# A hybrid decoder step: the split of the memory states per weight unit, the query pass ahead of the update, and the heads' work beside the projection on other places

## The chip, the cores and the metric

The kernel runs on one core of a Trainium2 chip. The metric is device time in microseconds (us) from start to end of one execution; lower is better. Engines are named TensorE (PE in the rows, PEld for its weight loads), VectorE (DVE), ScalarE (ACT), GpSimd (POOL) and SyncE (SP, which here only issues DMAs). Each engine works through its own instructions in the order in which the program emitted them.

## The reference

One layer on 576 tokens (512 of a new sequence, 64 of 8 running sequences with 8 new tokens each): a projection of 2048 inputs to 8 x 1024 columns and 8 gates, four heads of a chunked linear attention with a 256 x 256 state each, a gated convolution of width 31, an output projection and a layer norm. What matters for the change is the attention of the 8 running sequences, whose states come from memory (8 sequences x 4 heads, 256 x 256 float32 each):

```python
proj = jnp.einsum('bsd,de->bse', x, w_in) + b_in
q, k, v, o, zm, ga, gg, zc, ig, fg = jnp.split(proj, SPLITS, axis=-1)
...
s = jnp.einsum('bhtd,bhsd->bhts', qc, kc) * jnp.exp(dmat - m_t[..., None])
num = (w_inter[..., None] * jnp.einsum('bhtd,bhde->bhte', qc, C)     # queries meet the old state
       + jnp.einsum('bhts,bhse->bhte', s, vc))
...
C_new = decay[..., None, None] * C + jnp.einsum('bhs,bhsd,bhse->bhde', ws, kc, vc)   # update
```

## The kernel before, in words

**The projection sets the pace.** The 64 column blocks of 128 are made one after the other. The first three come from a loop of their own; the other 61 are called steps here and counted from 4. A step is 16 k-steps, one for each 128 rows of the weights, and a k-step is six matmuls (L185: float32 data in two parts, high and low, three products for each of two spans of tokens). Four k-steps share one weight unit of 512 columns, which `split` makes from the loaded `raw`: ScalarE the high part `whi` (L86), then VectorE the low part `wlo` (L87). It is called at the first k-step of a unit for the unit three ahead, and every second call then issues SyncE's load of another 512 KB of weights.

**All other work stands beside the projection**, at places written by hand: `at(s, k, f, ...)` has `f` emitted behind the matmuls of k-step k of step s (k may pass 16 and then counts on into later steps). A table sets the places for each head h, counted from a base step: `b_E` to `b_q` prepare the scores and the keys of the head (in the words of the change, its front), `b_rep` to `b_shT` are its back part.

**The states.** For each head the 8 states are taken in two groups of four (r = 0, 1). They lie in `Ct` tiles, 8 buffers, loaded by `c_load` (L377, SyncE). `c_split` cuts a state into three bfloat16 parts: c0 = round(C) (ScalarE, L401), the rest cr = C - c0 (VectorE, L407), c1 = round(cr) (ScalarE, L399), c2 = cr - c1 (VectorE, L404). It is called in two halves: part 0 emits the two ScalarE operations (c1 of the state before and c0 of this one), part 1, two k-steps later, the two of VectorE. One state follows another every four k-steps.

- `b_qC` (L640): 24 small matmuls of the queries with the three parts of four states, into one PSUM tile `mi`, which ScalarE then copies to `nsb` (L642).
- `b_sKV` (L652): 8 small matmuls, the update of four states, into three `mi` tiles and `ns`; VectorE adds them to the decayed states (`Ct`, L657) and GpSimd issues the stores (`o_cs`, L658).
- `b_sLN` part 0 (L667): the tokens' own scores times values, into one `mi`.
- `b_kT` (L502): the keys' transposes, two calls, one `mi` each.
- `c_next`: the loads of the next head's four states, into the buffers just stored.

There are three `mi` buffers, taken in turn by all of these. The parts c0 and c1 lie in the buffers that held the scores `Ph` and `Pl`; for head 0's second group alone they lie in four other buffers. In the first group the update (24 k-steps behind the first score product) stands ahead of `b_sLN` (26) and the query pass (28); in the second the update (49 for head 0, 46 for the others) stands ahead of the query pass (51).

**Also in these engines' queues:** `b_E` has GpSimd add the mask (L444) for the next head and ScalarE take the exponential (L439). `b_parts` splits q and k (L455, L456); the projection's result for k leaves PSUM through ScalarE (L201). At steps 25 to 30 the gates o and zm follow the heads: ScalarE's sigmoid (L799), for zm a VectorE product (L805), then a GpSimd product (L816, L820).

Of the kernel before, what the change touches and what calls it, by code (L numbers as in the profile page):

```python
# [7 lines left out]
F32 = mybir.dt.float32  # L8
F32R = mybir.dt.float32r
BF16 = mybir.dt.bfloat16  # L10
AF = mybir.ActivationFunctionType
# [3 lines left out]
P = 128  # L15
# [3 lines left out]
NB, T8 = 8, 8  # L19
# [37 lines left out]
def hybrid(ctx, tc, x0, wg0, wu, wgate, cpack, gpack, sct, hist, xres, lnp,  # L57
           o_y, o_ys, o_C, o_m, o_cs, o_ns, o_ms, o_cv, o_cvs):
    nc = tc.nc
    pe, act, dve, pool = nc.tensor, nc.scalar, nc.vector, nc.gpsimd  # L60
# [4 lines left out]
    def mt(shape, dt, name, tag=None, bufs=None):  # L65
        return main.tile(shape, dt, name=name, tag=tag or name, bufs=bufs or 1)
# [43 lines left out]
    CT = mt([P, NCT, NH], F32, "CT")  # L110
# [5 lines left out]
    hT = {}  # L116
# [37 lines left out]
    def mi(shape=(P, 512)):  # L154
        return psum.tile(list(shape), F32, name="mi", tag="mi", bufs=3)
# [111 lines left out]
    for k in range(KT):  # L267
        for n, x in enumerate((XH, XL)):
            for b in range(2):
                c0, c1 = SPANS[b]  # L270
# [99 lines left out]
    m = {}  # L370
    CS = {}
# [4 lines left out]
            CS[i] = m["t"]([P, 2, 258], F32, "Ct", bufs=8)  # L376
            nc.sync.dma_start(CS[i], sct[i])  # L377

    def c_split(h, r, j, part):

        i = NB * h + 4 * r
        if (j, part) == (0, 0):
            if (h, r) == (0, 1):
                for n in ("c0", "c1"):
                    m[n] = [mt([P, 2, 2, 258], BF16, n, tag="hT", bufs=8) for _ in range(2)]
            else:
                for n, tag in (("c0", "Ph"), ("c1", "Pl")):
                    c = m["t"]([P, 4, 2, 258], BF16, n, tag=tag)  # L390
                    m[n] = [c[:, :2], c[:, 2:]]
            c = m["t"]([P, 4, 2, 258], BF16, "c2")
            m["c2"] = [c[:, :2], c[:, 2:]]
            m["cr"] = {}
        c0, c1, c2 = (lambda j, c=m[n]: c[j // 2][:, j % 2] for n in ("c0", "c1", "c2"))
        cr = m["cr"]
        if part == 0:
            if j:
                act.activation(c1(j - 1), cr[j - 1], AF.Copy)  # L399
            if j < 4:  # L400
                act.activation(c0(j), CS[i + j], AF.Copy)  # L401
        else:
            if j:
                dve.tensor_sub(c2(j - 1), cr.pop(j - 1), c1(j - 1))  # L404
            if j < 4:
                cr[j] = m["t"]([P, 2, 258], F32, "cr", bufs=2)
                dve.tensor_sub(cr[j], CS[i + j], c0(j))  # L407

    def rb_load(h):
        m["RB"] = m["t"]([P, TOK + TS], F32, "RB")  # L410
# [181 lines left out]
    def rsqrt(r, v, a):  # L592

        act.activation(r, v, AF.Ln)
        act.activation(r, r, AF.Exp, scale=-0.5)
        dve.tensor_mul(a, r, r)
        dve.tensor_mul(a, a, v)
        dve.tensor_scalar(a, a, -0.5, 1.5, op0=OP.mult, op1=OP.add)
        dve.tensor_mul(r, r, a)

    def head_ln(num, rows, n, thr):
        t = m["t"]
        sm = t([rows, 5, n], F32, f"sm{n}")
        st = t([rows, n, 6], F32, f"st{n}")
        mv = t([rows, n, 2], F32, f"mv{n}")
        ad, rd, v, r, a = (sm[:, i] for i in range(5))
        den = num[:, :, 256]
        for i in range(n):
            dve.bn_stats(st[:, i], num[:, i, :DH])
        for i in range(n):  # L610
            dve.bn_aggr(mv[:, i], st[:, i])
        dve.scalar_tensor_tensor(ad, den, -1.0, den, op0=OP.mult, op1=OP.max)
        dve.tensor_tensor(ad, ad, thr, op=OP.max)
        dve.reciprocal(rd, ad)
        dve.tensor_mul(v, mv[:, :, 1], rd)
        dve.tensor_mul(v, v, rd)
        dve.tensor_scalar(v, v, EPS, None, op0=OP.add)
        rsqrt(r, v, a)
        dve.tensor_mul(r, r, rd)
        for i in range(n):  # L620
            dve.tensor_scalar(num[:, i, :DH], num[:, i, :DH], mv[:, i, 0:1], r[:, i:i + 1],
                              op0=OP.subtract, op1=OP.mult)
# [9 lines left out]
    def b_qC(h, r):  # L632

        if r == 0:
            m["nsb"] = m["t"]([P, 2, 258], F32, "nsb")
        ps = mi()
        for d in range(2):
            for n in ("c0", "c1", "c2"):
                for j in range(4):
                    pe.matmul(ps[32 * j:32 * j + 32, :258], lhsT=m["Q"][:, d, 4 * r + j], rhs=m[n][j // 2][:, j % 2, d],  # L640
                              start=d == 0 and n == "c0", stop=d == 1 and n == "c2")
        act.activation(m["nsb"][:, r], ps[:, :258], AF.Copy)  # L642
        if r:
            act.dma_start(nsd[h].rearrange("j i t r e -> (j i t) r e"), m["nsb"])
# [48 lines left out]
    def at(s, k, f, *a):  # L693
        s, k = s + k // KT, k % KT
        beside.setdefault((s, k), []).append((f, a))
# [4 lines left out]
    at(6, 9, open_m)  # L700
    for h in range(NH):
        b = 6 * h + 1
        o = 2 if h == 0 else 0
        for i in range(4):
            at(b + 3 + o, (14 + i if h == 0 else 7 + 2 * i), b_E, h, i)
        at(6 if h == 0 else b + 2, 11 if h == 0 else 5, b_parts, "q", h)
        at(6 if h == 0 else b + 4, 13 if h == 0 else 0, b_parts, "k", h)
        at(b + 4 + o, 5, b_QK, h, 0)
        at(b + 4 + o, 7, b_QK, h, 1)
        at(b + 4 + o, 7, b_rep, "k", h)  # L710
        at(b + 4 + o, 9, b_kT, h, 0)
        at(b + 4 + o, 11, b_kT, h, 1)
        at(b + 4 + o, 13, b_stk, "k", h)
        at(b + 4 + o, 14, b_q, h)
        if h + 1 < NH:
            at(b + 7, 0, rb_load, h + 1)
        o = 14 if h == 0 else 0
        at(b + 6, o + 1, b_rep, "v", h)
        at(b + 6, o + 2, b_vT, h, 0)
        at(b + 6, o + 4, b_vT, h, 1)  # L720
        at(b + 6, o + 6, b_stk, "v", h)
        at(b + 6, o + 7, b_vs, h)
        at(b + 6, o + 9, b_sn, h)
        o = (b + 6, o + 10)
        for I in range(4):
            at(o[0], o[1] + 2 * I, b_SV, h, I)
        at(o[0], o[1] + 7, lambda h: head_ln(m["num"], P, 4, CT[:, 14:18, h]), h)
        at(o[0], o[1] + 8, b_KV, h, 0)
        at(o[0], o[1] + 10, b_KV, h, 1)
        at(o[0], o[1] + 14, b_hT, h, 0)  # L730
        at(o[0], o[1] + 16, b_hT, h, 1)
        for r, k in enumerate((8, 30 if h == 0 else 29)):
            for j in range(5):
                for part in range(2):
                    at(o[0], o[1] + k + 4 * j + 2 * part, c_split, h, r, j, part)
            at(o[0], o[1] + (24, 49 if h == 0 else 46)[r], b_sKV, h, r)
            at(o[0], o[1] + (28, 51)[r], b_qC, h, r)
            at(o[0], o[1] + (33, 55)[r], c_next, h, r)
        at(o[0], o[1] + 26, b_sLN, h, 0)
        at(o[0], o[1] + 57, b_sLN, h, 1)  # L740
        at(o[0], o[1] + 66, b_sLN, h, 2)
        at(o[0], o[1] + 76, b_shT, h)


    cv = {}
# [170 lines left out]
    c0 = FIRST + ORDER.index(("zc", 0))  # L916
    c1 = c0 + 2
# [230 lines left out]
```

## Time and profile before

| | us |
|---|---|
| median of 3 runs (1144.4 to 1148.0) | 1146.7 |
| the profiled execution's own time | 1146.47 |
| its span, first to last instruction | 1144.8 |
| TensorE busy in the span | 1120.3 |
| VectorE, ScalarE, GpSimd busy | 740.9, 424.4, 148.6 |

TensorE is the engine to look at; the three others have idle time nearly everywhere. The profile counts a matmul as busy from its start to its modelled end, so TensorE's idle time is what it stood without any matmul; the granted clock has to be read beside it, since a matmul at half clock is busy as well.

### The profile page before, as it was taken

The numbers are of one execution on the slowest core, as the hardware profiler recorded it, in microseconds if no ns is written. First come the engines' busy times: TensorE is split into PE (matmuls) and PEld (weight loads), VectorE is DVE, ScalarE is ACT, GpSimd is POOL, SyncE is SP. The second block draws the span as 40 slices with busy tenths as digits, with TensorE's granted clock in tenths as the row PEclk, the third lists the DMA queues.
The fourth block names the chain that finished last, engine by engine and source line by source line (L and its number), as shares of the span: only waits on it lengthen the run. The fifth ranks groups of instructions, "written<-read, shape, count | busy, mean of one in ns | idle before, by whom it ended". The sixth has DMA issues, their size and how long they took to land.

```text
span 1144.8 us, 19958 instructions
## 1 busy us (share of the span) xinstructions
PE 1120.3 (98%) x8126; PEld 1072.1 (94%) x8126; DVE 740.9 (65%) x1250; ACT 424.4 (37%) x813; POOL 148.6 (13%) x217
## 2 busy tenths in 40 slices
PE   9999999999999998999999999999999999999996
PEld 8999998989999997999999999999999988888896
DVE  6385555555465545527899898999977871433448
ACT  5335553454445454422222222221336661221224
POOL 0021021021021002200011111111203310000004
PEclk9999999999999998999999999999999999999998
DMA  8114244244235222332233223222232245542228
GB/s 292 68 56 160 84 142 146 79 145 146 74 113 197 80 66 93 110 108 92 84 107 102 90 85 100 75 74 92 79 107 74 77 156 186 199 153 94 65 93 166
DMA packets 45228, 129.09 MB, mean 113 GB/s; under 512 B 5660, under 2 KB 11164, under 8 KB 44688
## 3 DMA queue, kind: packets, MB, share of 16 engines
q1 hardware_dynamic: 38880, 113.11, 29.6%
q0 software_dynamic: 4992, 12.94, 4.3%
q10 hardware_dynamic: 1264, 1.78, 0.5%
q8 instruction: 63, 1.03, 0.4%
q14 instruction: 29, 0.24, 0.1%
HBM read 110.91 MB, written 19.78 MB: 114 GB/s over the span
## 4 chain that ended last, share of the span: by engine, by line
PE 60%; DVE 1%; issue 0%; DVEq 0%
PE pp L185 42%; PE pp L1020 3%; PE pp L1021 3%; PE pp L1019 3%; PE mi L1020 2%; PE mi L1021 2%; PE mi L1019 2%; PE mi L1016 1%; PE mi L1015 1%; PE ns L1021 0%; PE ns L1019 0%; PE ns L1020 0%; DVE Ct L657 0%; DVE z L1052 0%; DVE c L404 0%; DVE z L1040 0%
## 5 line engine op out<-in xcount | busy, mean ns | idle before, releaser
L185 PE MATMUL pp<-xh,whi 128*128 128x256 f32 (+1 forms) x1952 | 422.8, 298 | 0.0
L185 PE MATMUL pp<-xl,whi 128*128 128x256 f32 (+1 forms) x1952 | 416.6, 295 | 0.0
L185 PE MATMUL pp<-xh,wlo 128*128 128x256 f32 (+1 forms) x1952 | 416.2, 295 | 0.0
L87 DVE TENSOR_TENSOR wlo<-raw,whi 128x512 fp32r<-128x512 f32 x300 | 220.8, 740 | 278.6 <-ACT whi L86 278.4
L185 PEld LDWEIGHTS pp<-xh,whi 128*128 128x128 f32 x1952 | 324.0, 189 | 5.2 <-issue 3.7
L185 PEld LDWEIGHTS pp<-xh,wlo 128*128 128x128 f32 x1952 | 327.6, 189 | 0.0
L185 PEld LDWEIGHTS pp<-xl,whi 128*128 128x128 f32 x1952 | 327.3, 189 | 0.0
L86 ACT ACTIVATE whi<-raw 128x512 fp32r<-128x512 f32 x300 | 187.6, 631 | 335.3 <-PE pp L185 175.8
L766 DVE SCALAR_TENSOR_TENSOR Y<-U,cp,Y 128x512 f32<-128x512 f32 x240 | 189.7, 790 | 5.3
L1020 PE MATMUL pp<-whi,mx 128*128 128x512 f32 (+1 forms) x128 | 46.9, 366 | 0.0
L1019 PE MATMUL pp<-whi,mx 128*128 128x512 f32 (+1 forms) x128 | 46.9, 366 | 0.0
L1021 PE MATMUL pp<-wlo,mx 128*128 128x512 f32 (+1 forms) x128 | 46.9, 366 | 0.0
L658 POOL DMA_DIRECT2D o_cs<-Ct x32 | 22.7, 779 | 170.8 <-DVE Ct L657 170.6
L1020 PE MATMUL mi<-whi,mx 128*128 128x512 f32 (+1 forms) x96 | 36.1, 376 | 0.0
L1019 PE MATMUL mi<-whi,mx 128*128 128x512 f32 (+1 forms) x96 | 36.0, 375 | 0.0
L1021 PE MATMUL mi<-wlo,mx 128*128 128x512 f32 (+1 forms) x96 | 36.0, 375 | 0.0
L399 ACT ACTIVATE c<-cr 128x516 bf16<-128x516 f32 x32 | 20.2, 632 | 42.0 <-DVE cr L407 42.0
L799 ACT ACTIVATE sg<-pp,cp 128x256 f32<-128x256 f32 (+1 forms) x48 | 21.3, 495 | 38.3 <-PE pp L185 38.2
L1021 PEld LDWEIGHTS pp<-wlo,mx 128*128 128x128 f32 x128 | 24.1, 188 | 4.3
L1019 PEld LDWEIGHTS pp<-whi,mx 128*128 128x128 f32 x128 | 24.0, 188 | 4.3
L1020 PEld LDWEIGHTS pp<-whi,mx 128*128 128x128 f32 x128 | 24.0, 188 | 4.3
L1047 POOL DMA_DIRECT2D o_ys<-zs x4 | 3.4, 1182 | 188.9 <-ACT zs L1046 188.9
(340 smaller groups left out, 1378.6 us busy)
## 6 DMA issues: line engine op xcount, KB each, us to landing
raw<-wu SPq DMA_DIRECT2D x154, 512.0 KB
Ct<-sct SPq DMA_DIRECT2D x32, 258.0 KB
o_cs<-Ct POOLq DMA_DIRECT2D x32, 256.0 KB, 3.2
xr<-x SPq DMA_DIRECT2D x16, 288.0 KB
z<-xres SPq DMA_DIRECT2D x8, 512.0 KB
wr<-wg SPq DMA_DIRECT2D x16, 192.0 KB
o_y<-z POOLq DMA_DIRECT2D x11, 256.0 KB, 7.0
o_y<-lnp SPq DMA_DIRECT2D x2, 1024.0 KB
```

What stands on the lines that cost most here:

```text
L86: act.activation(hi, r, AF.Copy)
L87: (eng or dve).tensor_tensor(out=lo, in0=r, in1=hi, op=OP.subtract)
L185: pe.matmul(out[b], lhsT=w, rhs=x[:, slice(*SPANS[b])], start=k == 0 and n < 2, stop=k == KT - 1 and n >= 4)
L399: act.activation(c1(j - 1), cr[j - 1], AF.Copy)
L658: pool.dma_start(o_cs[NB * h + b], c)
L766: dve.scalar_tensor_tensor(y, u, w, y, op0=OP.mult, op1=OP.add)
L799: act.activation(sg[:, c0:c1], ps, AF.Sigmoid, bias=b_in[:, c:c + 1])
L1015: pe.matmul(ps, lhsT=s_, rhs=hi, start=first, stop=False)
L1016: pe.matmul(ps, lhsT=s_, rhs=lo, start=False, stop=last)
L1019: pe.matmul(ps, lhsT=h_, rhs=hi, start=first, stop=False)
L1020: pe.matmul(ps, lhsT=l_, rhs=hi, start=False, stop=False)
L1021: pe.matmul(ps, lhsT=h_, rhs=lo, start=False, stop=last)
```

## The change

`c_split` loses its two halves: ScalarE's and VectorE's operations of a state are emitted together at one place, every four k-steps. The parts lie in whole tiles of four states, and head 0's second group uses the buffers of `Ph` and `Pl` like all others. The query pass stands 21 k-steps behind the group's first split, the update two k-steps behind it (23), the loads for the next head four behind the update (27). `b_sLN` part 0 stands ahead of both in the first group. For that the later heads' fronts (second `b_parts` to `b_q`) move back by 16, 8 and 4 k-steps for heads 1, 2 and 3, and the back parts by 8, 4 and 0; head 0 keeps its places there. No instruction of TensorE is added or taken away.

```diff
-    def c_split(h, r, j, part):
-        i = NB * h + 4 * r
-        if (j, part) == (0, 0):
-            if (h, r) == (0, 1):
-                for n in ("c0", "c1"):
-                    m[n] = [mt([P, 2, 2, 258], BF16, n, tag="hT", bufs=8) for _ in range(2)]
-            else:
...
+    def c_split(h, r, j):
+        if j == 0:
+            for n, tag in (("c0", "Ph"), ("c1", "Pl"), ("c2", "c2")):
+                m[n] = m["t"]([P, 4, 2, 258], BF16, n, tag=tag)
             m["cr"] = {}
...
+        if j:
+            act.activation(c1[:, j - 1], cr[j - 1], AF.Copy)
+        if j < 4:
+            act.activation(c0[:, j], CS[NB * h + 4 * r + j], AF.Copy)
+        if j:
+            dve.tensor_sub(c2[:, j - 1], cr.pop(j - 1), c1[:, j - 1])
+        if j < 4:
+            cr[j] = m["t"]([P, 2, 258], F32, "cr", bufs=2)
+            dve.tensor_sub(cr[j], CS[NB * h + 4 * r + j], c0[:, j])
...
+        o = (37, 21, 13, 9)[h]
+        at(b + 4, o, b_QK, h, 0)
...
+        o = (14, 8, 4, 0)[h]
+        at(b + 6, o + 1, b_rep, "v", h)
...
+        for r, k in enumerate((o + 8, o + 30)):
             for j in range(5):
...
-            at(o[0], o[1] + (24, 49 if h == 0 else 46)[r], b_sKV, h, r)
-            at(o[0], o[1] + (28, 51)[r], b_qC, h, r)
-            at(o[0], o[1] + (33, 55)[r], c_next, h, r)
+                at(b + 6, k + 4 * j, c_split, h, r, j)
+            at(b + 6, k + 21, b_qC, h, r)
+            at(b + 6, k + 23, b_sKV, h, r)
+            at(b + 6, k + 27, c_next, h, r)
```

TensorE, the second group of head 0. Before, the update (`mi<-vS,kS`) is followed at once by head 1's transposes (`mi<-ident,k`), and by the query pass (`Q`) two k-steps later:

```order
L185 MATMUL pp<-xh_66,wlo 128x256
L185 MATMUL pp<-xh_66,wlo 128x320
L652 MATMUL mi<-vS,kS 128x256 x3
L652 MATMUL ns<-vS,kS 128x256
...
L502 MATMUL mi<-ident,k 128x128 x4
L185 MATMUL pp<-xh_67,whi 128x256
...
L640 LDWEIGHTS Q
L640 MATMUL mi<-c_1987,Q 32x258
```

Now the query pass comes first, the update two k-steps behind it, and the next user of an `mi` is head 1's score product (`mi<-qh,kh`), eight k-steps on:

```order
L628 LDWEIGHTS Q
L628 MATMUL mi<-c_1969,Q 32x258
L185 MATMUL pp<-xh_68,whi 128x256
...
L185 MATMUL pp<-xh_68,wlo 128x256
L185 MATMUL pp<-xh_68,wlo 128x320
L640 MATMUL mi<-vS,kS 128x256 x3
L640 MATMUL ns<-vS,kS 128x256
...
L185 MATMUL pp<-xh_69,whi 128x256
...
L456 MATMUL mi<-qh,kh 128x512
```

So nothing that needs an `mi` is left close behind the update. VectorE, the first group of head 3 (`c_...<-cr` is c2, `cr<-Ct` the rest, `Ct<-Ct,dec` the update, `sg<-pp,cp,sg` the gate zm; the numbers behind a c are those of its tile). Before, the last rest of the group stands directly ahead of the update, and its last c2 behind the update and a weight unit:

```order
L805 SCALAR_TENSOR_TENSOR sg<-pp,cp,sg 128x320
L87 TENSOR_TENSOR wlo<-raw,whi 128x512
L404 TENSOR_TENSOR c_5184<-cr,c_5183 128x516
L407 TENSOR_TENSOR cr<-Ct,c_5182 128x516
L657 SCALAR_TENSOR_TENSOR Ct<-Ct,dec,mi 128x2x256 x3
L657 SCALAR_TENSOR_TENSOR Ct<-Ct,dec,ns 128x2x256
L87 TENSOR_TENSOR wlo<-raw,whi 128x512
L404 TENSOR_TENSOR c_5184<-cr,c_5183 128x516
L87 TENSOR_TENSOR wlo<-raw,whi 128x512
L407 TENSOR_TENSOR cr<-Ct,c_5443 128x516
```

Now, at the same place:

```order
L792 SCALAR_TENSOR_TENSOR sg<-pp,cp,sg 128x320
L87 TENSOR_TENSOR wlo<-raw,whi 128x512
L392 TENSOR_TENSOR c_5182<-cr,c_5181 128x516
L87 TENSOR_TENSOR wlo<-raw,whi 128x512 x2
L395 TENSOR_TENSOR cr<-Ct,c_5433 128x516
L645 SCALAR_TENSOR_TENSOR Ct<-Ct,dec,mi 128x2x256 x3
L645 SCALAR_TENSOR_TENSOR Ct<-Ct,dec,ns 128x2x256
L87 TENSOR_TENSOR wlo<-raw,whi 128x512
```

The last c2 has moved ahead of the update; between it and the update stand two weight units and the first rest of the next group.

## Rows read from the trace of the kernel before

**Rows 1.** The first section of the page, engine TensorE: busy time, share of the span, instructions.

```profile
PE 1120.3 (98%) x8126; PEld 1072.1 (94%) x8126; DVE 740.9 (65%) x1250; ACT 424.4 (37%) x813; POOL 148.6 (13%) x217
```

**Rows 2.** The view of who waited for whom, engine TensorE, whole span. Columns: tile and line that waited, what it waited for, us in total, times, the longest.

```profile
PE mi L667 <- DVE Ct L657: 6.4, 3, 4.8
PE mi L640 <- DVE c L404: 3.1, 5, 1.2
PE mi L502 <- DVE Ct L657: 2.4, 1, 2.4
PE ns L220 <- DVE warm L217: 1.5, 1, 1.5
```

**Rows 3.** Busy time by stretch, two stretches of the span (one of the conv stage, and the end). Columns: start and end, length, then for each engine us busy and instructions, then PEclk (the granted clock, 1.00 is full speed), DMA share, GB/s.

```profile
600.00:700.00 100.00, 100.00 (x762) 100.00 (x761) 94.00 (x129) 24.04 (x43) 12.70 (x20) 1.00 0.29 95
1100.00:1145.00 45.00, 33.81 (x283) 33.60 (x281) 33.05 (x78) 15.85 (x31) 13.15 (x15) 0.91 0.62 121
```

**Rows 4.** The same view, microsecond by microsecond behind the two longest waits, and one stretch of ten microseconds with a short wait in it.

```profile
230.00:240.00 10.00, 9.20 (x70) 8.28 (x69) 5.47 (x9) 5.85 (x12) 0.70 (x2) 1.00 0.20 64
...
177.00:178.00 1.00, 1.00 (x7) 1.00 (x8) 1.00 (x2) 0.32 (x1) 0.84 (x2) 0.76 0.95 356
178.00:179.00 1.00, 1.00 (x7) 1.00 (x6) 1.00 (x3) 0.15 (x1) 1.00 (x2) 0.50 0.81 291
179.00:180.00 1.00, 1.00 (x6) 1.00 (x5) 0.46 (x2) 0.47 (x1) 1.00 (x3) 0.50 0.78 258
180.00:181.00 1.00, 1.00 (x18) 0.55 (x21) 0.26 (x1) 0.00 (x0) 0.62 (x2) 0.53 0.92 299
...
439.00:440.00 1.00, 0.89 (x2) 0.28 (x2) 1.00 (x3) 0.58 (x2) 0.65 (x1) 0.50 0.00 0
440.00:441.00 1.00, 1.00 (x4) 0.84 (x4) 1.00 (x3) 0.38 (x1) 1.00 (x3) 0.50 0.41 160
441.00:442.00 1.00, 1.00 (x7) 1.00 (x6) 1.00 (x3) 0.00 (x0) 1.00 (x2) 0.50 0.85 283
442.00:443.00 1.00, 1.00 (x6) 1.00 (x5) 0.23 (x1) 0.00 (x0) 0.18 (x1) 0.50 0.81 266
443.00:444.00 1.00, 1.00 (x22) 0.58 (x25) 0.00 (x0) 0.00 (x0) 0.00 (x0) 0.62 0.98 336
```

**Rows 5.** The instructions in order of time, head 3, first group of four states, around its update. Columns: start in us, duration, engine, line, operation, out<-in, shape, count; in brackets the idle time before and what ended it.

```profile
427.39 0.63 ACT L399 ACTIVATE c<-cr 128x516 bf16<-128x516 f32 x1 [0.82 <-DVE cr L407]
...
430.32 0.69 DVE L407 TENSOR_TENSOR cr<-Ct,c 128x516 f32<-128x516 f32 x1
...
431.05 0.63 ACT L399 ACTIVATE c<-cr 128x516 bf16<-128x516 f32 x1 [1.97 <-DVE cr L407]
...
432.00 0.19 PEld L652 LDWEIGHTS mi<-vS,kS 32*128 32x128 f32 x3 [0.16 <-issue]
...
434.44 0.94 DVE L805 SCALAR_TENSOR_TENSOR sg<-pp,cp,sg 128x256 f32<-128x256 f32 x2 [3.43 <-ACT sg L799]
...
435.53 1.71 POOL L820 TENSOR_TENSOR hT<-hT,sg 128x576 f32<-128x576 f32 x1 [20.40 <-DVE sg L805]
435.90 1.89 DVE L404 TENSOR_TENSOR c<-cr,c 128x516 bf16<-128x516 f32 x1
...
438.32 2.05 DVE L657 SCALAR_TENSOR_TENSOR Ct<-Ct,dec,mi 128x512 f32<-128x512 f32 x3
...
439.11 1.12 PE L667 MATMUL mi<-vs,Es 64*64 64x258 f32 x2 [4.82 <-DVE Ct L657]
```

**Rows 6.** The same view at head 0's second group, whose update stands just ahead of head 1's transposes of k.

```profile
174.05 0.39 PE L652 MATMUL mi<-vS,kS 32*128 32x256 f32 x3
...
176.92 0.66 PE L502 MATMUL mi<-ident,k 128*128 128x128 f32 x4 [2.37 <-DVE Ct L657]
```

**Rows 7.** Groups of instructions by line with shapes apart, 100 to 500 us: busy time and mean ns of one, then the idle time before them and what ended it.

```profile
L87 DVE TENSOR_TENSOR wlo<-raw,whi 128x512 fp32r<-128x512 f32 x97 | 69.9, 725 | 121.1 <-ACT whi L86 121.0
L86 ACT ACTIVATE whi<-raw 128x512 fp32r<-128x512 f32 x97 | 60.4, 627 | 26.8 <-PE pp L185 17.5 <-DMA raw<-wu 8.2 <-ACT whi L86 0.7
L404 DVE TENSOR_TENSOR c<-cr,c 128x516 bf16<-128x516 f32 x32 | 23.2, 726 | 1.0 <-ACT c L399 1.0
...
L407 DVE TENSOR_TENSOR cr<-Ct,c 128x516 f32<-128x516 f32 x32 | 22.5, 705 | 0.0
L399 ACT ACTIVATE c<-cr 128x516 bf16<-128x516 f32 x32 | 20.2, 632 | 42.0 <-DVE cr L407 42.0
...
L201 ACT ACTIVATE k<-pp,bk 128x320 f32<-128x320 f32 x6 | 3.1, 515 | 0.0
```

**Rows 8.** GpSimd and ScalarE around head 0's and head 1's first update, in order of time: the four stores of the new states (its DMA issues), then the four mask sums of the next head and, of ScalarE, three of its exponentials; and, from the view of line 658 alone, how long a store takes from issue to landing.

```profile
149.74 2.90 POOL L658 DMA_DIRECT2D o_cs<-Ct  x4 [42.27 <-DVE Ct L657]
...
152.30 2.16 POOL L444 TENSOR_TENSOR E<-RB,cmask 128x128 f32<-128x128 f32 x4
...
155.97 0.98 ACT L439 ACTIVATE E<-RB,CT 128x128 f32<-128x128 f32 x3
...
241.86 3.55 POOL L444 TENSOR_TENSOR E<-RB,cmask 128x128 f32<-128x128 f32 x4
...
DMA to landing us min/median/max: 2.5/3.2/5.7
```

**Rows 9.** The waits of SyncE's DMA queue, same columns as rows 2.

```profile
SPq L377 <- DMA o_cs<-Ct: 6.1, 4, 3.8
```

More of the change, by code (lines that the diff above doesn't have):

```diff
@@ L377, in c_load @@
             nc.sync.dma_start(CS[i], sct[i])
-    def c_split(h, r, j, part):
-        i = NB * h + 4 * r
-        if (j, part) == (0, 0):
-            if (h, r) == (0, 1):
-                for n in ("c0", "c1"):
-                    m[n] = [mt([P, 2, 2, 258], BF16, n, tag="hT", bufs=8) for _ in range(2)]
-            else:
[L389 to L393, printed above, removed]
-            m["cr"] = {}
[L395 to L407, printed above, removed]
+    def c_split(h, r, j):
+        if j == 0:
+            for n, tag in (("c0", "Ph"), ("c1", "Pl"), ("c2", "c2")):
+                m[n] = m["t"]([P, 4, 2, 258], BF16, n, tag=tag)
+            m["cr"] = {}
+        c0, c1, c2, cr = (m[n] for n in ("c0", "c1", "c2", "cr"))
+        if j:
[7 more added lines that the diff above has]
+            dve.tensor_sub(cr[j], CS[NB * h + 4 * r + j], c0[:, j])
     def rb_load(h):
@@ L639, in b_qC @@
                 for j in range(4):
-                    pe.matmul(ps[32 * j:32 * j + 32, :258], lhsT=m["Q"][:, d, 4 * r + j], rhs=m[n][j // 2][:, j % 2, d],
+                    pe.matmul(ps[32 * j:32 * j + 32, :258], lhsT=m["Q"][:, d, 4 * r + j], rhs=m[n][:, j, d],
                               start=d == 0 and n == "c0", stop=d == 1 and n == "c2")
@@ L702, in hybrid @@
         b = 6 * h + 1
-        o = 2 if h == 0 else 0
         for i in range(4):
-            at(b + 3 + o, (14 + i if h == 0 else 7 + 2 * i), b_E, h, i)
+            at(b + 3, (46 + i if h == 0 else 7 + 2 * i), b_E, h, i)
         at(6 if h == 0 else b + 2, 11 if h == 0 else 5, b_parts, "q", h)
[L707 to L714, printed above, removed]
+        at(6 if h == 0 else b + 4, (13, 17, 10, 6)[h], b_parts, "k", h)
+        o = (37, 21, 13, 9)[h]
+        at(b + 4, o, b_QK, h, 0)
+        at(b + 4, o + 2, b_QK, h, 1)
+        at(b + 4, o + 2, b_rep, "k", h)
+        at(b + 4, o + 4, b_kT, h, 0)
+        at(b + 4, o + 6, b_kT, h, 1)
+        at(b + 4, o + 8, b_stk, "k", h)
+        at(b + 4, o + 9, b_q, h)
         if h + 1 < NH:
             at(b + 7, 0, rb_load, h + 1)
-        o = 14 if h == 0 else 0
+        o = (14, 8, 4, 0)[h]
         at(b + 6, o + 1, b_rep, "v", h)
@@ L723, in hybrid @@
         at(b + 6, o + 9, b_sn, h)
-        o = (b + 6, o + 10)
+        o += 10
         for I in range(4):
[L726 to L732, printed above, removed]
-            for j in range(5):
-                for part in range(2):
-                    at(o[0], o[1] + k + 4 * j + 2 * part, c_split, h, r, j, part)
-            at(o[0], o[1] + (24, 49 if h == 0 else 46)[r], b_sKV, h, r)
-            at(o[0], o[1] + (28, 51)[r], b_qC, h, r)
-            at(o[0], o[1] + (33, 55)[r], c_next, h, r)
[L739 to L742, printed above, removed]
+            at(b + 6, o + 2 * I, b_SV, h, I)
+        at(b + 6, o + 7, lambda h: head_ln(m["num"], P, 4, CT[:, 14:18, h]), h)
+        at(b + 6, o + 8, b_KV, h, 0)
+        at(b + 6, o + 10, b_KV, h, 1)
+        at(b + 6, o + 14, b_hT, h, 0)
+        at(b + 6, o + 16, b_hT, h, 1)
+        for r, k in enumerate((o + 8, o + 30)):
+            for j in range(5):
+                at(b + 6, k + 4 * j, c_split, h, r, j)
+            at(b + 6, k + 21, b_qC, h, r)
+            at(b + 6, k + 23, b_sKV, h, r)
+            at(b + 6, k + 27, c_next, h, r)
+        at(b + 6, o + 25, b_sLN, h, 0)
+        at(b + 6, o + 58, b_sLN, h, 1)
+        at(b + 6, o + 67, b_sLN, h, 2)
+        at(b + 6, o + 77, b_shT, h)
     cv = {}
```

## The prediction

> **What bounds the kernel now.** I read the engines' totals first: TensorE is busy 1120.3 of 1144.8 us [rows 1], so 24.5 us are idle. The waits of TensorE name 11.9 us in the middle [rows 2]: 6.4 for an `mi` that VectorE's update (L657) still holds ahead of the tokens' own scores (L667), 2.4 for the same ahead of head 1's transposes (L502), and 3.1 for the last c2 (L404) ahead of the query pass (L640). The remaining 12.6 us lie at the two ends: 1.5 before the first matmul [rows 2] and 45 - 33.81 = 11.2 in the last stretch [rows 3]. In the conv stage TensorE has no gap, at 762 matmuls in 100 us [rows 3]: a matmul each 0.131 us, a k-step of six 0.79, four 3.15.
>
> The second place to look is the granted clock. Behind the two longest waits, of 2.37 us [rows 6] and 4.82 us [rows 5], it stands at 0.50, the 1.2 GHz level, while matmuls run; in a stretch with a wait of 0.8 it stays at 1.00 [rows 4]. What is lost is busy time x (1 - clock). Behind the first: 0.24 + 0.50 + 0.50 + 0.47 = 1.7 us. Behind the second: 0.89 x 0.5 + 0.5 + 0.5 + 0.5 + 0.38 = 2.3 us. Together 4.0 us that no list of waits shows.
>
> Third, why VectorE is late there. At the update of head 3's first group the chain reads [rows 5]: c1 starts at 427.39 and the next c1 at 431.05, so a state takes 3.66 us, not the 3.15 of four k-steps. Nothing is overloaded: ScalarE has 3 x 0.63 and VectorE 3 x 0.72 us of work per state [rows 7]. But each waits for the other in turn: high part, low part, c2, rest, c1, c0; c1 alone waited 42.0 us for the rest in all [rows 7]. Then the zm gate (0.94), c2 stretched to 1.89 beside GpSimd's product (1.71) and the rest stand ahead of the update, which starts 438.32 - 432.00 = 6.3 us behind its matmuls.
>
> **The change, part by part.** TensorE's instructions are the same in number and shape, so its work costs nothing new.
>
> *Splits together.* Per state ScalarE now runs high part, c1, c0 and VectorE low part, c2, rest, and c2 of one state overlaps c0 of the next. The loop that cannot overlap is rest -> c1 -> c0 -> rest: 0.63 + 0.63 + 0.71 = 2.0 us [rows 7], under 3.15. So the splits keep up with TensorE, where they lost 0.5 us per state.
>
> *Query pass ahead.* The last c2 is emitted five k-steps (3.9 us) ahead of the pass, where there were two in a first group, and no update stands between. Behind a unit's start it needs a high part, c1 and c2, 0.63 + 0.63 + 0.73 = 2.0, plus a low part's 0.73 at worst: 2.7, under 3.9. At head 3's first group the zm gate still falls in between. The step ends three k-steps ahead of the old update, at 432.0 - 2.4 = 429.6. ScalarE came to the sigmoids only behind the c1 of 431.05 and the c0 behind that (about 432.2), 2.6 late, and the gate began at 434.4, 4.8 behind the step's end. Without the lateness it begins at 2.2 and ends at 3.2; the low part ends at 3.9, c2 at 4.6, or at 5.8 if it again takes 1.89. The pass stands eight k-steps behind the step's end, at 6.3. No wait, by 0.5 at the least. Gain: all 3.1.
>
> *Own scores ahead of the update.* They no longer ask for an `mi` that the update holds: 6.4 gone, with the 2.3 of clock. *Fronts later.* Behind each second group's update the next user of an `mi` is the next head's score product, eight or six k-steps on (6.3 or 4.7 us); four update sums take 2.05 + 0.74 = 2.8 [rows 5]. So 2.4 gone, with 1.7 of clock. What is late next there is kl: behind the update's 0.4 + 2.8, a low part and one half of kl at 0.7 each end at 4.6, while the third score matmul comes at 0.4 + 4.7 + 0.5 = 5.6. It hides by 1.0.
>
> *What the update now stands behind.* It takes as its third `mi` the one that the query pass filled, two k-steps before (1.6 us). ScalarE's copy (0.4) must come within them; nothing that waits for anything else is queued ahead of it. Cost 0.
>
> *Loads for the next head.* They come four k-steps behind the update (3.2 us), where it was nine or six. A store begins some 1.2 us behind the update and the four take 2.9 to issue, 3.2 to land [rows 8]: SyncE stands at the loads from 3.6 to about 7.6, 4 us, where its longest such wait was 3.8 [rows 9]. Behind it waits a load of weights at most; that has twelve k-steps (9.5 us) until its split, and the unit another three units. Cost 0; the limit is a rival below.
>
> *Head 0's second group* has the one tight place. Its first update now stands at the same k-step as GpSimd's mask sums for head 1, and GpSimd has the four stores first: from the update's start 1.2 + 2.9 = 4.1, then the first sum, 0.54 (2.16 / 4) to 1.85 us [rows 8], so 4.6 to 6.0. ScalarE reaches head 1's exponentials at about 2 and stands there. From 5.3 it has ten exponentials at 0.33, seven c0 or c1 and three high parts at 0.63, two copies of k at 0.5 [rows 7, 8]: 10.6, to 15.9, and VectorE's c2 to 16.6. The query pass is 20 k-steps on, 0.4 + 15.8 = 16.2, and wants that c2 at 16.5. On the edge: between nothing (rows start 0.54 apart where they follow each other, under the 0.63 of one) and 2.4 us (the mask sums' late end, 0.7, another 0.5 of GpSimd's slow sums and a c2 of 1.89 instead of 0.73). I take 0.4, near the lower end, since VectorE is nearly empty in that stretch.
>
> **Sum.** The profiled execution took 1146.5, 0.2 below the median of the runs, which I neglect. 1146.5 - (6.4 + 3.1 + 2.4) - (1.7 + 2.3) + 0.4 = 1131.0. What comes behind step 30 shifts as a whole, its places being counted in k-steps.
>
> A rule bears on the tight place. In the trace c2 took 1.89 us where GpSimd's product of 1.71 ran, 0.73 otherwise [rows 5, 7]. The Trainium skill, "SBUF — State Buffer", section "SBUF: two separate sides", says that GpSimd shares a port pair with VectorE operations that have two SBUF inputs, as an exclusive lock: the later one fully blocks. That speaks against moving mask sums onto splits. By it the sums and VectorE's splits would queue up whole, and the sum would be the first rival's time; by the rows it is 1131.0, because VectorE has little to do while ScalarE stands.
>
> **The rivals.**
> 1. The tight place waits in earnest: 2.4 us for c2, with a clock loss like the 1.7 behind the wait of 2.37: 4.1, so 1131 + 4 = 1135. For it: the slow mask sum of 1.85 and the slow c2 of 1.89. Against: each needs the two engines to meet. 12%.
> 2. The long wait stays: head 3's gate still delays c2 and only the name of who waits changes. 4.8 + 2.3 = 7.1, so 1138. For it: table load, sigmoid, gate and GpSimd's product are where they were. Against: the 0.5 us of room above. 6%.
> 3. The gain is given back in the conv stage, where VectorE is busy 94.00 of 100 us [rows 3]: 1146. Against: TensorE is busy 100.00 there, and taps are emitted per k-step, so VectorE sees the same rate. 5%.
> 4. Slower: SyncE's stand at the next head's loads starves the weights. It happens six times; if the stores landed so late that loads came more than 9.5 us late and the units ran dry, each would be a wait like the longest, 4.8 + 2.3 = 7.1. From three of them on (21 us) the change loses: 1131 + 21 = 1152. For it: the wait is longer and more frequent than before. Against: a stand of 4 us, landing at worst in 5.7 [rows 8], and no wait of TensorE for a weight part anywhere now [rows 2]. 5%.
>
> **How the numbers follow.** The forecast has 72%. It spans 1128.5 to 1134: runs of one kernel lie from 1144.4 to 1148.0, about 2 on either side, and small waits of a microsecond may add up. With rival 1 the range is 1128.5 to 1137.5 and holds 84%. About 0.3% (3.4 us) is what a measurement can tell from no change: faster is the forecast with rivals 1 and 2, 0.90; same is rival 3, 0.05; slower is rival 4, 0.05.
>
> **What would show it.** Right: no wait of an `mi` user for the update in the list of TensorE's waits, at most a microsecond for c2, TensorE idle some 12.6 to 13.5 us in all, and the clock at 1.00 from 100 to 500 us; c1 starts 3.15 us apart in the splits. Wrong: a wait for c2 at head 0's second group (rival 1), a wait at the gate of head 3 (rival 2), TensorE gaps between 600 and 800 us (rival 3), a wait of a projection matmul for a weight part (rival 4).

## The result, and the profile after

The changed kernel takes 1130.32 us in the median of 4 runs (1129.64 to 1130.53), the kernel before 1147.35 in the runs beside it: a ratio of 0.9855, 95% interval 0.9837 to 0.9874. The forecast was 1131.0, in a range of 1128.5 to 1137.5.

The head of the page of the changed kernel, and the row that [rows 1] shows of the kernel before:

```profile
span 1128.8 us, 19953 instructions
...
PE 1116.0 (99%) x8126; PEld 1070.0 (95%) x8126; DVE 744.3 (66%) x1250; ACT 423.6 (38%) x813; POOL 151.2 (13%) x217
```

The whole list of what TensorE waited for, with the same columns as [rows 2]:

```profile
PE ns L220 <- DVE warm L217: 1.5, 1, 1.5
```

Busy time, granted clock and DMA by stretch, the columns of [rows 3]:

```profile
100.00:200.00 100.00, 100.00 (x801) 96.94 (x800) 59.24 (x126) 47.40 (x103) 12.91 (x25) 1.00 0.34 112
...
400.00:500.00 100.00, 100.00 (x800) 97.84 (x799) 48.80 (x98) 45.29 (x81) 15.48 (x15) 1.00 0.32 105
...
600.00:700.00 100.00, 100.00 (x762) 100.00 (x762) 91.53 (x127) 23.18 (x41) 12.65 (x19) 1.00 0.29 94
...
1100.00:1129.00 29.00, 17.69 (x148) 17.48 (x146) 23.32 (x53) 11.93 (x23) 13.15 (x15) 0.87 0.88 164
```

The span is 16.0 us shorter, and the two readings add up to it. TensorE's idle time fell from 1144.8 - 1120.3 = 24.5 to 1128.8 - 1116.0 = 12.8 us, 11.7 less: all three lines of waits for an `mi` or for c2 are gone, and none has come. Its busy time fell by 4.3 us with the same 8126 matmuls. Most of that are the 4.0 us that the prediction put down to the fallen clock [rows 4]: it now stands at 1.00 in every stretch between 100 and 500 us. The other 0.3 is less than two executions of the changed kernel differ by (1116.0 us busy here, 1115.1 in experiment 10). What is idle still lies at the two ends, 1.5 us and 29 - 17.69 = 11.3.

The splits of head 3's first group in order of time, the engines that [rows 5] shows:

```profile
414.59 0.64 ACT L388 ACTIVATE c<-cr 128x516 bf16<-128x516 f32 x1 [1.45 <-DVE cr L395]
...
417.77 0.62 ACT L388 ACTIVATE c<-cr 128x516 bf16<-128x516 f32 x1
...
419.76 0.63 ACT L388 ACTIVATE c<-cr 128x516 bf16<-128x516 f32 x1 [0.32 <-DVE cr L395]
...
423.16 0.94 DVE L792 SCALAR_TENSOR_TENSOR sg<-pp,cp,sg 128x256 f32<-128x256 f32 x2 [1.43 <-ACT sg L786]
...
424.25 1.73 POOL L807 TENSOR_TENSOR hT<-hT,sg 128x576 f32<-128x576 f32 x1 [17.67 <-DVE sg L792]
424.62 1.92 DVE L392 TENSOR_TENSOR c<-cr,c 128x516 bf16<-128x516 f32 x1
...
428.16 0.85 PE L628 MATMUL mi<-c,Q 128*32 128x258 bf16 x24
```

c1 starts at 414.59, 417.77 and 419.76, 3.2 and 2.0 us apart, so the splits keep TensorE's pace of 3.15 us and even catch up where they were late. The zm gate still delays c2, and GpSimd's product still stretches it to 1.92 us. But it ends at 426.5, and the query pass comes at 428.16.

The place that the prediction called tight, head 0's second group with head 1's mask sums: GpSimd's stores (first row) and sums, ScalarE's exponential, two c2 and the query pass.

```profile
156.40 2.18 POOL L646 DMA_DIRECT2D o_cs<-Ct  x3 [48.73 <-DVE Ct L645]
...
158.96 2.07 POOL L432 TENSOR_TENSOR E<-RB,cmask 128x128 f32<-128x128 f32 x4
...
159.83 0.40 ACT L427 ACTIVATE E<-E,CT 128x128 f32<-128x128 f32 x1 [4.53 <-POOL E L432]
...
161.66 0.70 DVE L392 TENSOR_TENSOR c<-cr,c 128x516 bf16<-128x516 f32 x1 [2.99 <-ACT c L388]
...
169.66 0.70 DVE L392 TENSOR_TENSOR c<-cr,c 128x516 bf16<-128x516 f32 x1
...
171.27 0.84 PE L628 MATMUL mi<-c,Q 128*32 128x258 bf16 x24
```

ScalarE does stand 4.53 us until GpSimd's sums have followed the stores. The last c2 ends at 170.4, and the pass starts at 171.27: 0.9 us to spare.

SyncE's waits for the stores, the columns of [rows 9]: longer and more frequent, as expected, and no matmul waits for a weight behind them. Over the six groups of loads they are 23.6 / 6 = 3.9 us a group on average, where the prediction had 4.

```profile
SPq L377 <- DMA o_cs<-Ct: 23.6, 18, 5.7
```

### The profile page after: what moved, and what is told of

It reads as the page before. It is cut to its first block, busy times and chain, and to the rows that moved or that the text cites. A ratio compares the mean times of both kernels' runs of the same rounds, so it can differ in the third digit from the quotient of the medians.

```text
span 1128.8 us, 19953 instructions
## 1 busy us (share of the span) xinstructions
PE 1116.0 (99%) x8126; PEld 1070.0 (95%) x8126; DVE 744.3 (66%) x1250; ACT 423.6 (38%) x813; POOL 151.2 (13%) x217
## 4 chain that ended last, share of the span: by engine, by line
PE 98%; DVE 1%; DMA 0%; ACT 0%; issue 0%; SPq 0%; DVEq 0%
PE pp L185 71%; PE pp L1006 3%; PE pp L1008 3%; PE pp L1007 3%; PE mi L1007 2%; PE mi L1008 2%; PE mi L1006 2%; PE mi L456 1%; PE mi L1003 1%; PE mi L1002 1%; PE mi L566 1%; PE mi L185 1%; PE mi L574 1%; PE mi L628 1%; PE ns L1008 1%; PE ns L1006 1%
## 5 line engine op out<-in xcount | busy, mean ns | idle before, releaser
L392 DVE TENSOR_TENSOR c<-cr,c 128x516 bf16<-128x516 f32 x32 | 24.2, 755 | 14.4 <-ACT c L388 13.9
```

Of the source, the lines that this page charges most:

```text
L392: dve.tensor_sub(c2[:, j - 1], cr.pop(j - 1), c1[:, j - 1])
```

## The experiments

**1. The splits together, alone.** The kernel before, with its two halves at one place:

```diff
-                    at(o[0], o[1] + k + 4 * j + 2 * part, c_split, h, r, j, part)
+                    at(o[0], o[1] + k + 4 * j, c_split, h, r, j, part)
```

> The kernel before with one part of the change alone: a state's ScalarE and VectorE operations are emitted together, all places stay. Theory (the waits come from VectorE reaching the update and the last c2 late, because the halves make ScalarE and VectorE wait for each other by turns): the last c2 is now ahead of the update in both groups, so the 3.1 us for c2 and the two short waits of 0.8 for an mi go; at head 3 the zm gate still delays c2, so about 1.9 of the 4.8 stay, and about 1.8 of the 2.4 ahead of head 1's transposes. 1146.5 - 3.1 - 1.6 - 2.9 - 0.6 = 1138.3, less 2.3 and 1.7 where the clock does not fall: 1134 to 1138.5. Rival (the places of update and query pass make the waits, the halves are harmless): the list of waits stays as it was, 1144 to 1147.

Measured: 1135.88 us, ratio 0.9906 (0.9886 to 0.9925). TensorE's waits in the middle:

```profile
PE mi L667 <- DVE Ct L657: 2.0, 2, 1.5
...
PE mi L502 <- DVE Ct L657: 1.0, 1, 1.0
```

The 3.1 us for c2 are gone without any other place having moved, and 6.4 have become 2.0. So this one line brings 11 of the 17 us. The reason shows in head 3's first group: c1 now starts 3.2 us apart, where it was 3.66 in [rows 5], and the one behind it follows after 2.0:

```profile
415.92 0.64 ACT L399 ACTIVATE c<-cr 128x516 bf16<-128x516 f32 x1 [1.45 <-DVE cr L407]
...
419.11 0.62 ACT L399 ACTIVATE c<-cr 128x516 bf16<-128x516 f32 x1
```

The clock stood at 1.00 around the remaining wait at head 3 (1.5 us), in the profiled execution. Its mean granted clock was 0.997; the other three executions had 0.994 to 0.995, so in those it may have fallen.

```profile
425.00:430.00 5.00, 3.45 (x28) 2.70 (x25) 5.00 (x7) 1.52 (x3) 2.90 (x3) 1.00 0.28 105
```

**2. The new places, with the splits in halves.** The changed kernel with the two halves of `c_split` back:

```diff
+                for part in range(2):
-                at(b + 6, k + 4 * j, c_split, h, r, j)
+                    at(b + 6, k + 4 * j + 2 * part, c_split, h, r, j, part)
```

> The changed kernel with the splits in halves again (VectorE's half two k-steps behind ScalarE's), all new places kept. Theory: the splits again take 3.66 us a state where they stand as in heads 1 to 3 before, and at head 3's first group the rest and c1 of the last state come behind the zm gate, so the query pass waits there about 4 us for c2 with a clock loss of about 2, elsewhere at most 0.7 at a time: 1135 to 1139. Rival (the new places alone bring the gain): no such wait, 1130 to 1132.

Measured: 1142.20 us, ratio 0.9962 (0.9949 to 0.9975), above the range of the theory. TensorE waits for c1 and c2:

```profile
PE mi L628 <- ACT c L388: 4.7, 2, 2.7
PE mi L628 <- DVE c L392: 3.4, 2, 1.8
```

Two places make these rows: head 3's first group with 2.0 + 1.8, as expected, and head 0's second with 2.7 + 1.6, where at most 0.7 was expected. At head 3 the pace of before is back, c1 starts 3.65 us apart:

```profile
424.84 0.63 ACT L388 ACTIVATE c<-cr 128x516 bf16<-128x516 f32 x1 [0.82 <-DVE cr L395]
...
428.49 0.64 ACT L388 ACTIVATE c<-cr 128x516 bf16<-128x516 f32 x1 [1.97 <-DVE cr L395]
```

The other is the tight place: ScalarE comes late from the mask sums, and with the halves it doesn't catch up. c1 starts there 4.5, 4.4 and 3.7 us apart; in the changed kernel it is 3.6, 2.3 and 2.1. The new places alone are worth less than a third of the gain.

**3. Head 1's front later, alone.** The kernel before with head 1's front 16 k-steps later (the split of k, its first piece, 17, as in the changed kernel; head 2's moves by 10 and head 3's by 6 there):

```diff
+        f = 16 if h == 1 else 0
-        at(b + 4 + o, 5, b_QK, h, 0)
+        at(b + 4 + o, 5 + f, b_QK, h, 0)
...
```

> The kernel before with one part of the change alone: head 1's front (the split of k to the query products) stands 16 k-steps later, as in the changed kernel; its back part and all else stay. Theory: only the wait of 2.4 us ahead of head 1's transposes goes, with 1.7 of clock: 1146.5 - 4.1 = 1142.4, between 1141.5 and 1143.5; the other two lines of the list of waits stay at 6.4 and 3.1. Rival (the update's sums are late for whoever comes next, so the wait moves on to the score product): 1145 to 1147.

Measured: 1151.70 us, ratio 1.0044 (1.0028 to 1.0059): slower, and both accounts wrong. The wait ahead of the transposes (L502) is gone, as the theory said, but another has come:

```profile
PE mi L667 <- DVE Ct L657: 6.4, 3, 4.8
PE mi L520 <- ACT v L203: 4.0, 1, 4.0
PE mi L640 <- DVE c L404: 3.1, 5, 1.1
...
PE mi L640 <- DVE Ct L657: 1.2, 1, 1.2
```

L520 are the transposes of v at the start of the back part. The last row is head 0's second query pass: it is now the first behind the update that asks for an `mi`, so half of the 2.4 us moved on, though not to the score product. The instructions in order of time show what stands ahead of ScalarE's copy of v:

```profile
191.50 0.48 DVE L507 SCALAR_TENSOR_TENSOR kwl<-mi,CT,kwh 128x256 fp32r<-128x256 f32 x1 [0.54 <-ACT kwh L506]
...
191.90 1.32 DVE L679 TENSOR_TENSOR nums<-nums,n 64x258 f32<-64x258 f32 x3
...
196.62 0.47 DVE L507 SCALAR_TENSOR_TENSOR kwl<-mi,CT,kwh 128x256 fp32r<-128x256 f32 x1
...
197.73 0.27 PE L520 MATMUL mi<-ident,v 128*128 128x128 f32 x1
...
201.50 0.87 ACT L203 ACTIVATE v<-pp,cp 128x256 f32<-128x256 f32 x2
...
202.01 0.90 PE L520 MATMUL mi<-ident,v 128*128 128x128 f32 x3 [4.01 <-ACT v L203]
```

VectorE has head 0's layer norm (from 191.90) between the halves of head 1's keys (the first kwl at 191.50, the next at 196.62); ScalarE waits for VectorE in the keys, and comes to the copy of v at 201.50. The transposes stand three k-steps (2.4 us) behind the end of v's projection, at 197.73; so the copy is some 6 us behind that end and 3.8 behind the first transpose. The clock fell as well, and stood at 0.50 from 202 to 207 us.

**4. The back parts unmoved.** That wait says that the 8 and 4 k-steps of the back parts are no decoration. The changed kernel without them:

```diff
-        o = (14, 8, 4, 0)[h]
+        o = (14, 0, 0, 0)[h]
```

> The changed kernel with the back parts of heads 1 and 2 at their old places (shifts 14, 0, 0, 0 instead of 14, 8, 4, 0); the fronts stay late. It tests what head 1's front alone showed: behind the late front ScalarE and VectorE still work on head 0's layer norm and head 1's keys when the transposes of v come. Theory: head 1's first transpose of v waits some 4 us for ScalarE's copy of v, with about 3 of clock; head 2 has 12 k-steps between and waits nothing: 1136 to 1138.5. Rival (the wait in that run came from the old places of head 0's update and query pass): no wait, 1129 to 1131.

Measured: 1137.35 us, ratio 0.9904 (0.9890 to 0.9917). TensorE's waits:

```profile
PE mi L508 <- ACT v L203: 4.0, 1, 4.0
...
PE mi L673 <- DVE kwl L495: 1.3, 1, 1.3
```

The time lies in the range of the theory. The wait of 4.0 for v is there, in the changed kernel too, so head 0's old places are not its cause. A second wait was not expected: 1.3 at head 1's last transposes (L673), which with the unmoved back part come upon the late keys of head 2 (kwl, L495).

**5. Head 1's front and back later, the rest as before.**

```diff
-        o = 14 if h == 0 else 0
+        o = (14, 8, 0, 0)[h]
```

> The kernel before with head 1's front 16 and its back part 8 k-steps later, all else as before. Theory: the wait of 2.4 ahead of head 1's transposes goes with its 1.7 of clock, and no wait for v takes its place, since the back part's 8 k-steps (6.3 us) cover 4.0: 1146.7 - 4.1 = 1142.6, between 1141 and 1144; the waits of 6.4 and 3.1 stay. Rival (the late head 1 runs into something else): 1145 or more.

(On top of experiment 3.) Measured: 1147.90 us, ratio 1.0006 (0.9994 to 1.0018): the rival was right.

```profile
PE mi L640 <- DVE c L404: 5.7, 5, 3.3
PE mi L667 <- DVE Ct L657: 5.7, 2, 4.8
```

The waits for transposes and for v are both gone, as the theory has it. But a wait of 3.3 for c2 came at head 1's second group, whose query pass now meets head 2's front:

```profile
264.01 2.06 DVE L657 SCALAR_TENSOR_TENSOR Ct<-Ct,dec,mi 128x512 f32<-128x512 f32 x3
...
266.64 1.29 DVE L456 TENSOR_TENSOR kl<-k,kh 128x512 fp32r<-128x512 f32 x2
...
267.84 0.69 DVE L404 TENSOR_TENSOR c<-cr,c 128x516 bf16<-128x516 f32 x1
...
268.58 0.60 PE L640 MATMUL mi<-c,Q 128*32 128x258 bf16 x13 [3.27 <-DVE c L404]
```

The last c2 stands behind the update and behind the split of head 2's keys (kl, L456). So a head that moves pushes onto the next one. This is shown for head 2 behind head 1, with the splits in halves and the update ahead of the pass; whether the changed kernel needs the whole row of 16, 8 and 4 was not tested.

**6. The own scores ahead of the update, alone.**

```diff
-        at(o[0], o[1] + 26, b_sLN, h, 0)
+        at(o[0], o[1] + 23, b_sLN, h, 0)
```

> The kernel before with one part of the change alone: the tokens' own scores stand ahead of the first group's update (one k-step, instead of two behind it). Theory (VectorE is late, and whoever comes next waits for it): the waits of 0.8 move to the query pass, which comes earlier by as much; at head 3 the pass meets an update that starts 6.3 us late and a c2 behind it and waits 5 us and more, with the clock loss: 1143.5 to 1147. Rival (the own scores stand at the wrong place, moving them removes what the list of waits puts down to them): 6.4 and 2.3 less, 1137 to 1139.

Measured: 1147.05 us, ratio 1.0001 (0.9990 to 1.0011), the upper end of the theory. TensorE's waits:

```profile
PE mi L640 <- DVE c L404: 6.6, 7, 1.2
PE mi L502 <- DVE Ct L657: 2.4, 1, 2.4
PE mi L652 <- ACT nums L669: 2.1, 1, 2.1
```

11.1 us instead of 11.9, under other names. The largest line of the list of before is emptied, and nothing is gained: what was late is VectorE, not the product that stood first in line for it. The long wait that the theory named at head 3 is split there between 2.1 us (the update's third `mi`, which the own scores' copy to `nums` still holds) and 1.2 for c2.

**7. The update back ahead of the query pass, splits together.**

```diff
-            at(b + 6, k + 23, b_sKV, h, r)
+            at(b + 6, k + 19, b_sKV, h, r)
```

> The changed kernel with the update back ahead of the query pass: update 19, query pass 21 k-steps behind the group's first split, splits together. Theory: with the last c2 ready in time, VectorE starts on the update at once; the query pass needs the mi that the first update sum frees (1.2 us behind the update's matmuls) two k-steps (1.6 us) later, so nothing waits, also not at head 3, where c2 ends 5.5 and the first sum 6.3 us behind the step's end and the pass comes at 6.7: 1130 to 1131. Rival (the order is what counts): the waits of the query pass for c2 or for an mi are back in all eight groups, 3 us and more, 1133 to 1138.

Measured: 1132.11 us (1131.33 to 1132.45), ratio 0.9871 (0.9855 to 0.9888), 1.1 above the range of the theory. TensorE has no wait in the middle at all. The order, then, brings no more than 2 us, and these are no wait; experiment 10 comes back to them.

**8. The query pass four k-steps earlier.**

```diff
-            at(b + 6, k + 21, b_qC, h, r)
-            at(b + 6, k + 23, b_sKV, h, r)
+            at(b + 6, k + 17, b_qC, h, r)
+            at(b + 6, k + 19, b_sKV, h, r)
```

> The changed kernel with the query pass four k-steps earlier, one behind the last split (17), update two behind it (19). It measures how much of the distance is needed. Theory: in the trace of the changed kernel the last c2 ends 0.9 us ahead of the pass at head 0's second group and 1.6 ahead at head 3's first; 3.15 us less leaves waits of about 2.3 (with a clock loss near 1.7) and 1.6 there, and 0.5 to 1.2 in the other six: 9 to 11 us, 1138 to 1142. Rival (the distance is not needed, the last c2 is ready anyway): 1130 to 1132.

Measured: 1136.39 us, ratio 0.9904 (0.9881 to 0.9926): between the two accounts.

```profile
PE mi L628 <- DVE c L392: 3.2, 4, 1.8
```

The distance is needed, but in four groups of eight only: 1.8 us at head 3's first group (1.6 expected), 0.5 at head 0's first, 0.5 and 0.3 at the second groups of heads 1 and 2. Where the theory had most, at head 0's second group, nothing waits. The edit moved head 0's first update too, and with it GpSimd's stores, so the mask sums came earlier and ScalarE stood for them 0.80 us instead of 4.53:

```profile
157.77 0.40 ACT L427 ACTIVATE E<-E,CT 128x128 f32<-128x128 f32 x1 [0.80 <-POOL E L432]
```

I had counted the four k-steps at the pass and not at the stores. Behind the wait of 1.8 the clock fell to 0.50, the 1.2 GHz level, in the profiled execution:

```profile
429.00:431.00 2.00, 2.00 (x21) 1.40 (x21) 0.00 (x0) 1.21 (x3) 0.00 (x0) 0.92 0.34 131
431.00:433.00 2.00, 2.00 (x12) 1.72 (x15) 0.69 (x1) 0.08 (x1) 0.00 (x0) 0.50 0.00 0
```

**9. The loads of the next head's states at once.**

```diff
-            at(b + 6, k + 27, c_next, h, r)
+            at(b + 6, k + 23, c_next, h, r)
```

> The changed kernel with the loads of the next head's states right behind the update instead of four k-steps later. It lengthens what the slower rival fears: SyncE stands at each group of loads from the update on until the stores have landed, about 7 us instead of 4, six times, and a load of weights may stand behind it. Theory: weights have more than 9.5 us of room, nothing waits: 1130 to 1131. Rival (the weights starve): waits of projection matmuls for a weight part, 1134 or more.

Measured: 1129.22 us, ratio 0.9846 (0.9833 to 0.9860), 0.8 below the range of the theory. SyncE stands at these loads for 56.0 us instead of 23.6, 9.3 us a group where 7 were expected, once for 9.6, and no matmul waits for a weight:

```profile
SPq L377 <- DMA o_cs<-Ct: 56.0, 24, 9.6
```

**10. The changed kernel again.**

> The changed kernel once more, on the chip of the two runs beside it, to have its spread from one set of executions to another: 1129 to 1132 by the two variants of it in which TensorE had no wait either (1132.1 with the update first, 1129.2 with the loads at once). If it comes within 1 of 1130.3 in all executions, these two differ from it by more than spread.

Measured: 1129.41 us (1128.82 to 1130.59), ratio 0.9837 (0.9824 to 0.9851). So the changed kernel does not stay within 1 us of 1130.3: its lowest execution is 1.5 below. The run with the loads at once lies inside this spread. The run with the update first lies 0.7 us and more outside. Its TensorE is idle for as long (12.5 against 12.6 us); the difference is busy time, and it shows in the conv stage, where neither kernel differs from the other. The same stretch, the changed kernel and then the one with the update first (after the length: TensorE busy us and matmuls):

```profile
520.00:820.00 300.00, 300.00 (x2280) 300.00 (x2280) 280.15 (x371) 74.37 (x136) 39.13 (x44) 1.00 0.27 89
```

```profile
520.00:820.00 300.00, 300.00 (x2272) 300.00 (x2271) 279.52 (x370) 74.50 (x136) 39.79 (x44) 1.00 0.26 88
```

With TensorE busy throughout and the clock at 1.00 it did 2280 matmuls in one and 2272 in the other, 0.35% apart. Such a difference comes up within one kernel too: from 800 to 900 us, the changed kernel in the execution of the result and then in the one of this run.

```profile
800.00:900.00 100.00, 100.00 (x755) 100.00 (x754) 79.91 (x106) 50.00 (x83) 24.56 (x15) 1.00 0.27 89
```

```profile
800.00:900.00 100.00, 100.00 (x761) 100.00 (x760) 80.16 (x107) 50.28 (x83) 24.60 (x15) 1.00 0.27 90
```

So the rate can change between executions without any change of the program. What makes it I could not settle; but all four executions with the update first lie above all nine of the changed kernel, so whether the order of update and query pass is worth anything below 2 us stays open.

## Why the prediction was right

**The sum.** Terms and measured: waits of 6.4, 3.1 and 2.4, together 11.9, against 11.7 of idle time; clock 4.0, against 4.3 of busy time (0.3 of it within what executions differ by); a new wait of 0.4 at the tight place, against none. Of the forecast's 0.7 us above the result this 0.4 is the largest part, 0.1 is what the other terms together came out larger (16.0 against 15.9), and the rest is within the spread of the runs. The sum asked only that all three waits go, not which part takes away which; two of its three headings for them were wrong, and that this cost nothing is luck.

**Splits together.** The argument from the rows (3.66 us a state, each engine waiting for the other in turn, neither full) is shown by experiments 1 and 2: that part alone gives 11 us, and without it the other parts give about 5. Emitting VectorE's half at ScalarE's place also emits it two k-steps earlier, so the gain might come from the distance alone. It does not: at head 3's first group the last c2 is emitted three k-steps ahead of the pass with the halves (experiment 2), and the pass waited 2.0 + 1.8 us; without them one k-step was enough for a wait of 1.8 (experiment 8). What brings the 5.6 us from experiment 1 to the changed kernel was not taken apart further; 3.0 of it are the waits that experiment 1 left.

**Query pass ahead.** The text put the whole 3.1 us under this heading. That was the wrong heading: experiment 1 removes them with the update still in front, and experiment 7 has no wait either. What the new place does give is distance: with four k-steps less (experiment 8) 3.2 us of waits come back, and the clock falls again. The room at head 3 was put at 0.5 us with a c2 of 1.89; it is 1.6 with 1.92, because the splits come to the gate early.

**Own scores ahead of the update.** That the 6.4 us would go was right, that this move takes them away was not: alone it moves them (experiment 6), and splits together leave only 2.0 of them (experiment 1). Whether this move then takes the 2.0, or the update's new place does, was not tested.

**Fronts later.** "So 2.4 gone, with 1.7 of clock" is right for its wait (experiment 3), of which the splits together alone take 1.4 (experiment 1), but was an incomplete step. It looked at what comes next for the update (kl), not at what comes next for the later front itself. Behind it stands the back part, and without the 8 k-steps of that the move costs 4.0 us of waiting for v and the clock loss behind it (experiments 3 and 4); with them, but without the same move of the next head, it costs a wait of 3.3 for c2 (experiment 5, in the kernel before). The prediction named the back parts' shifts in no term, though the sum rests on them.

**The tight place.** Sized at 16.6 us, where the pass wants its c2 at 16.5, it waits for nothing, by 0.9 us; its lower bound held. The mechanism is there: with halves it costs 4.3 us (experiment 2). Of the lock that the Trainium skill tells of ("SBUF — State Buffer", section "SBUF: two separate sides") the trace shows the condition missing, as the forecast had it: VectorE has a gap of 2.99 us around GpSimd's sums. Where the two do meet, at head 3, c2 takes 1.92 us instead of some 0.7, and ends 0.6 us behind GpSimd's product, which agrees with it.

**The rivals.** First and second: no wait of TensorE at either place. Third: the conv stage stays at 762 matmuls in 100 us, and 16 us less in front of it are 16 us less at the end. Fourth: SyncE's longest stand of 9.6 us in experiment 9 starves nothing.

## What to carry to other kernels

When the list of waits names a product that waits for an engine with idle time, look at what that engine waited for, not at the product's place: two engines that hand a value back and forth can fall behind a pace at which neither is full, and emitting their operations so that one value's step overlaps the next one's was worth more here than all the moves. Moving the first waiter alone gained nothing; moving one block later cost 5 us alone, and still gained nothing with its own second part moved as well. A wait of TensorE can cost more than its length: read the granted clock behind it and add busy time x (1 - clock).

## What was not expected of the hardware

In the profiled executions the clock fell behind waits of 1.8 us (experiment 8), 2.37 and 4.82 us [rows 4, 5, 6], but not behind one of 1.5 (experiment 1) or 0.8 [rows 4]. Other executions of the same kernels may have gone otherwise: their mean clocks were 0.994 to 0.996 (experiment 8) and 0.994 to 0.995 (experiment 1). And with the clock at 1.00 and no gap, TensorE's rate of matmuls in the conv stage was 2271 or 2272 in 300 us in four of the profiled executions (experiments 1, 5, 6 and 7) and 2280 or 2281 in the eight others, of kernels that don't differ there; the cause is open.
